# mLSTM projections: the o of heads 2 and 3 as one block of 512 columns, with its own order of token tiles

## The chip, the core and the metric

The kernel runs on one core of a Trainium2 chip as one program. A core has engines that run side by side, each through its own queue in order: TensorE (PE, matrix products; its weight loads are shown as PEld), VectorE (DVE), ScalarE (ACT), GpSimd (POOL) and SyncE (SP). SP and POOL here mostly issue DMA transfers between the device memory and the on-chip memory. TensorE writes its products to PSUM, from where ScalarE or VectorE must take them before the bank is used again. The metric is the device time of one execution in microseconds, the median over several runs.

## What is computed

A two-layer network over 1024 latent tokens and 256 context tokens, 1280 rows of width 1024. The first layer has neighbourhood attention heads beside four bidirectional mLSTM heads of dimension 256; the second has HGRN2 heads. The change touches only the mLSTM part of the first layer, whose reference is, cut to what matters:

```python
qa, ka, va, za, qb, kb, vb, ob, zb, g = _split_cols(h @ w_in, AB_SIZES)   # ob, zb: 1024 columns, 256 a head
hb_l, hb_c = _mlstm_bidir(mb_l, mb_c, need_ctx)          # two scans over chunks, forwards and backwards, summed
def merge(oa, hb, za, ob, zb):
    hb = jnp.swapaxes(hb, 1, 2) * jax.nn.sigmoid(_heads(ob, ML_HEADS))
    hb = _rms(hb, h_norm.reshape(ML_HEADS, ML_DIM))
    yb = hb.reshape(hb.shape[:2] + (ML_WIDTH,)) * jax.nn.silu(zb)
    ...
    return jnp.concatenate([ya, yb], axis=-1) @ w_out
```

So for each head the recurrence gives an h, which is gated by the projection o, normalized, and gated again by the projection z. o and z of a head are needed only when a token tile of its h is finished.

## The kernel before

**Projections.** The modulated input h stands transposed in on-chip memory as a high part and a low part (hh, hl), and so do the weights (`wblock`, L77 to L111: each piece of 128x512 is loaded by SP into one of three raw buffers `wraw`, L100, then ScalarE casts the high part, L71, and VectorE subtracts to get the low part, L72). `dense` (L124 to L130) makes each product of three matmuls per block of 128 rows of the inner dimension: high by high (L127), low by high or high by low (L128, L129). With an inner dimension of 1024 that is 24 matmuls for a tile.

A narrow block, `proj_out` (L304), projects onto 256 columns, one head. Its weights are four pieces. It takes two token tiles of 128 rows into one PSUM bank, 48 matmuls of 256 columns, evicts both at once, and POOL stores 256 KB to `md` (L319). Its order of tiles is the pairs that begin with 8, 4, 2, 6, 0. A wide block, `proj_wide` (L274), projects onto 512 columns, two heads side by side. Its weights are eight pieces: six go into the ring `w` of six slots, two into the ring `wx` of two slots. It takes one token tile at a time, 24 matmuls of 512 columns, evicts it and stores the halves for the two heads (L289). In both, the eviction goes through the ring `ev` of two buffers; for o it is a tanh on ScalarE (`gate_o`, L323), for z a tanh and a multiplication on VectorE (`gate_z`, L327), for v a copy (L283). Both use the two PSUM banks `mm`.

`ml_ahead(part, h, pool)` (L338) chooses: with a pool a part other than q and k is projected wide for heads h and h + 1, without one it is narrow. `md` holds v, o and z of the four heads.

**Recurrence.** `ml_rec` (L499) runs for the four heads one after the other, and `ml_load` of the next head is woven in. A head has ten chunks of 128 tokens in two directions: 20 steps, 80 in all. A step's first matmul is L534 (acc from mSD), the others are L544 (acc from mqc and the state mC) and L553 (the state's update from mvw), all of 258 columns. VectorE and ScalarE make mSD, mqc, mvw and update mC in between. Each tile of tokens is finished when the second direction has passed it: the forward direction goes 8, 9, 0, 1, ... 7, the backward one 9, 8, 7, ... 0, so the tiles are finished as 9, 8, 4, 3, 5, 2, 6, 1, 7, 0. For a finished tile `ml_out` (L593) loads o and z from `md` (L596, two buffers `mloz`, SP), gates by o (L599, VectorE), squares (L602, ScalarE), takes the root on GpSimd (L153, L155), scales and gates by z (L604, L605). `ml_yt` (L607) then transposes it (L612, TensorE; L613, ScalarE) and stores it to `yd` for the output projection.

**Output projection.** `out_ahead` (L835) makes the first half of the inner dimension (the attention heads' part of y, ready long before) for the second 512 output columns, ten token tiles of 24 matmuls of 512 columns (L829 to L831, in `out_sum`). Its weights use the six `w` slots and two slots `wo`; the `wo` slots, and its y pieces but for the first tile, stand where hh and hl stood, so they wait for the last projection. y of its first tile is loaded into the `ev` buffers (L812) and split into `wx` slots. Then `out_tile` (L847) adds the second half.

**Who sets the order.** The program is written in the order above, but a scheduler decides in which order the instructions stand on each engine's queue. It takes what is ready by its own timeline, highest priority first. Projections inside `with self.filler()` have a priority behind everything else, so they are placed into the gaps that the recurrence leaves on TensorE. Among themselves they keep the order of the program: v of heads 0 and 1 wide, z of head 1, v of heads 2 and 3 wide, o of head 2, z of head 2, o of head 3, z of head 3 (L1224 to L1229). On the chip each engine runs its queue in the order so fixed.

Of the kernel before, what the change touches and what calls it, by code (L numbers as in the profile page):

```python
# [43 lines left out]
class Prog:  # L44
# [293 lines left out]
    def ml_ahead(self, part, h, pool=None, mark=False):  # L338
        i = "qkvoz".index(part)
        c0 = (4 + i) * D + h * 256  # L340
        gate = {"o": self.gate_o, "z": self.gate_z}.get(part)
        if part in "qk":
            self.proj_out_tr(c0, self.mt[4 * i + h])
        elif pool:
            pair = self.md[4 * (i - 2) + h : 4 * (i - 2) + h + 2]
            self.proj_wide(c0, lambda s: pair[:, s, :].rearrange("h p f -> p h f"), pool, [8, 9] + list(range(8)), gate)
        else:

            self.proj_out(c0, self.md[4 * (i - 2) + h], gate, (8, 4, 2, 6, 0), mark)
# [762 lines left out]
    def build(self):  # L1112
        tc, nc, a = self.tc, self.nc, self.a
        dma = nc.sync.dma_start
        with ExitStack() as es:
# [88 lines left out]
            with tc.tile_pool(name="na", bufs=2) as pool, self.pp.phase(tq=1, s=2, acc=1):  # L1204
                qk = self.na_qk(0, pool)
                z = self.na_z(0, pool)
                ahead = [("k", 0), ("q", 1), ("k", 1), ("q", 2), ("k", 2), ("q", 3)]
                for p2 in range(8):
                    self.na_attn(p2, qk, z, pool)
                    if p2 < 7:  # L1210
# [5 lines left out]
                        z = self.na_z(p2 + 1, pool)  # L1216
# [5 lines left out]
            with tc.tile_pool(name="ml", bufs=2) as pool, self.pp.phase(s=2, acc=2):  # L1222
                with self.filler():
                    self.ml_ahead("v", 0, pool)  # L1224
                    self.ml_ahead("z", 1)
                    self.ml_ahead("v", 2, pool)
                    for h in (2, 3):
                        for part in "oz":
                            self.ml_ahead(part, h)  # L1229
                self.mask = self.t(pool, [P, 2, P], F32, "mmask", 1)  # L1230
                dma(out=self.mask, in_=a["mmask"])
                st, parts = self.ml_load(0, pool)
                for ld in parts:
                    ld()
                for h in range(4):
                    nxt, parts = self.ml_load(h + 1, pool) if h < 3 else (None, None)
                    self.ml_rec(h, st, pool, parts)
                    st = nxt

                ys = [self.out_y(0, 0, self.yd, pool, 2, (self.wp, "ev", 2), "wx")]  # L1240
                right.close()

                wr = es.enter_context(ExitStack())
                yp = wr.enter_context(tc.tile_pool(name="oy", bufs=1, side="right"))
                wo = (yp, "wo", 8)
                acc, w2 = self.out_ahead(
                    a["woab"], NT, self.yd, yp, ([(self.wp, "w", 6)] * 6 + [wo] * 2, [wo] * 8),
                    [[self.wp, 3, "wraw"]] * 2, ys,
                )
# [59 lines left out]
            with l1:  # L1309
                pool = l1.enter_context(tc.tile_pool(name="hg", bufs=2))  # L1310
# [3 lines left out]
                for h in range(16):  # L1314
# [5 lines left out]
                    z = st["z"]  # L1320
# [11 lines left out]
            with tc.tile_pool(name="op1", bufs=2) as op, ExitStack() as wl:  # L1332
# [3 lines left out]
                for b, w in ((1, w2), (0, w1)):  # L1336
                    self.gate_bc(1, op, 1, b)
                    for tt in range(8):
# [3 lines left out]
                            part=acc[:, tt, :] if b else None,  # L1342
# [142 lines left out]
```

## Time and profile before

| | us |
|---|---|
| runs of before: median, lowest, highest of 3 | 3489.57, 3488.38, 3491.35 |
| the profiled execution: its time, its span | 3489.28, 3487.5 |
| recurrence and fillers, about | 1150 to 1620 |
| first output projection (`out_ahead`) begins | 1622.8 |

The profile is of one execution. Times count from the start of its span. A row of the timeline gives start, length, engine, line, operation, out<-in, shapes, a count, and in brackets the idle time of the engine before it and what ended that. TensorE records of 258 columns come twice for each matmul in the program. TensorE's records overlap, since the matmuls are pipelined, so a matmul's price is read from the distance of starts, not from its length. PEclk is the share of the full TensorE clock that was granted.

### The profile page before, as it was taken

Reading aid. Unit: us, or ns where it says so; the run is one execution under the profiler, and the core shown is the slowest. Engines: PE = TensorE matmul, PEld = TensorE weight load, DVE = VectorE, ACT = ScalarE, POOL = GpSimd, SP = SyncE. Lnnn points to the kernel's source line nnn. Section 1 sums busy time; section 2 is a strip of 40 time slices with the busy share of each in tenths; the row PEclk is TensorE's granted clock in tenths of the full one; section 3 lists DMA queues with packets and bytes.
Section 4 is the critical chain, followed back from the end, with each engine's and each line's share of the span. In section 5 each row is a group of like instructions: output and inputs, shape, how many; then the busy total and the mean of one; then the engine's idle time right before and its main releaser. Section 6 shows DMA issues by size and latency. Waiting matters only on the chain.

```text
span 3487.5 us, 61004 instructions
## 1 busy us (share of the span) xinstructions
PE 3451.0 (99%) x23004; PEld 3073.9 (88%) x23004; DVE 2229.8 (64%) x5407; ACT 1478.8 (42%) x3557; POOL 522.5 (15%) x824
## 2 busy tenths in 40 slices
PE   8999999999999999999999999999999999999999
PEld 5679998889989888997888999999999999999887
DVE  4546665666655566886566666666666667666753
ACT  5445554555443444554354333333333333333431
POOL 2222222222211112222000000000100000100000
PEclk9999999999999999999999999999999999999999
DMA  5542222322233433434752111111111111111263
GB/s 204 173 134 57 82 77 72 91 80 76 78 90 101 140 118 122 138 120 148 215 166 67 37 37 34 37 37 37 35 36 35 35 36 37 37 36 33 85 195 116
DMA packets 321029, 303.98 MB, mean 87 GB/s; under 512 B 28168, under 2 KB 277192, under 8 KB 320736
## 3 DMA queue, kind: packets, MB, share of 16 engines
q1 hardware_dynamic: 288576, 216.47, 21.2%
q0 software_dynamic: 32160, 83.61, 7.1%
q8 instruction: 182, 2.98, 0.4%
q14 instruction: 111, 0.91, 0.1%
HBM read 240.52 MB, written 59.30 MB: 86 GB/s over the span
## 4 chain that ended last, share of the span: by engine, by line
PE 88%; issue 5%; DMA 3%; DVE 1%; ACT 1%; POOL 1%; SPq 0%; POOLq 0%; ACTq 0%; DVEq 0%
PE mm L128 19%; PE mm L127 19%; PE mm L129 19%; PE s L1015 5%; PE acc L772 2%; PE tr L752 2%; PE mm L829 2%; PE mm L830 2%; PE mm L831 2%; PE s L553 2%; PE acc L544 2%; PE acc L534 1%; PE acc L1075 1%; PE acc L1077 1%; PE acc L1076 1%
## 5 line engine op out<-in xcount | busy, mean ns | idle before, releaser
L128 PE MATMUL mm<-hl,wh 128*128 128x512 f32 (+1 forms) x1600 | 587.8, 367 | 0.0
L127 PE MATMUL mm<-hh,wh 128*128 128x512 f32 (+1 forms) x1600 | 584.1, 365 | 0.0
L129 PE MATMUL mm<-hh,wl 128*128 128x512 f32 (+1 forms) x1600 | 583.2, 365 | 0.0
L129 PE MATMUL mm<-wh,hl 128*128 128x256 f32 (+1 forms) x1620 | 496.6, 307 | 0.3 <-DVE hl L261 0.3
L127 PE MATMUL mm<-wh,hh 128*128 128x256 f32 (+1 forms) x1620 | 495.0, 306 | 1.4 <-ACT ev L316 0.6
L128 PE MATMUL mm<-wl,hh 128*128 128x256 f32 (+1 forms) x1620 | 495.4, 306 | 0.0
L129 PEld LDWEIGHTS mm<-hh,wl 128*128 128x128 f32 x1600 | 301.6, 189 | 45.7 <-issue 0.6
L127 PEld LDWEIGHTS mm<-hh,wh 128*128 128x128 f32 x1600 | 301.3, 188 | 45.2 <-issue 0.2
L128 PEld LDWEIGHTS mm<-hl,wh 128*128 128x128 f32 x1600 | 301.7, 189 | 43.3 <-issue 0.2
L127 PEld LDWEIGHTS mm<-wh,hh 128*128 128x128 f32 x1620 | 305.9, 189 | 15.1 <-issue 1.1
L128 PEld LDWEIGHTS mm<-wl,hh 128*128 128x128 f32 x1620 | 306.0, 189 | 13.6 <-issue 2.9
L129 PEld LDWEIGHTS mm<-wh,hl 128*128 128x128 f32 x1620 | 305.8, 189 | 13.7 <-issue 1.4
L127 PE MATMUL mm<-wzh,hh 128*128 128x256 f32 x1024 | 299.1, 292 | 0.4 <-ACT gz L921 0.4
L129 PE MATMUL mm<-wzh,hl 128*128 128x256 f32 x1024 | 291.5, 285 | 0.0
L128 PE MATMUL mm<-wzl,hh 128*128 128x256 f32 x1024 | 291.5, 285 | 0.0
L71 ACT CAST wh<-wraw 128x512 fp32r<-128x512 f32 x242 | 148.5, 620 | 242.8 <-PE mm L128 187.6
L72 DVE TENSOR_TENSOR wl<-wraw,wh 128x512 fp32r<-128x512 f32 x242 | 165.5, 689 | 93.0 <-ACT wh L71 82.6
L1015 PE MATMUL s<-gQ,gksel 128*128 128x128 f32 x1536 | 204.2, 276 | 0.0
L1010 ACT COPY gksel<-gK 128x512 f32<-128x512 f32 x192 | 120.3, 635 | 183.9 <-PE s L1015 152.7
L127 PEld LDWEIGHTS mm<-wzh,hh 128*128 128x128 f32 x1024 | 193.9, 189 | 0.6 <-ACT gz L921 0.6
L128 PEld LDWEIGHTS mm<-wzl,hh 128*128 128x128 f32 x1024 | 193.4, 189 | 0.0
L129 PEld LDWEIGHTS mm<-wzh,hl 128*128 128x128 f32 x1024 | 192.4, 188 | 0.0
(359 smaller groups left out, 7721.7 us busy)
## 6 DMA issues: line engine op xcount, KB each, us to landing
wraw<-yd SPq DMA_DIRECT2D x142, 256.0 KB
wraw<-in_wab_dram SPq DMA_DIRECT2D x112, 256.0 KB
wraw<-in_wc_dram SPq DMA_DIRECT2D x96, 256.0 KB
adar<-in_wada_dram POOLq DMA_DIRECT2D x32, 512.0 KB, 4.4
wraw<-in_wc_dram SPq DMA_DIRECT2D x128, 128.0 KB
md<-ev POOLq DMA_DIRECT2D x60, 256.0 KB, 2.9
mloz<-md SPq DMA_DIRECT2D x40, 256.0 KB
adar<-in_wada_dram SPq DMA_DIRECT2D x16, 512.0 KB
```

The costliest lines, as they stand in the source:

```text
L71: nc.scalar.copy(hi, x)
L72: nc.vector.tensor_tensor(out=lo, in0=x, in1=hi.bitcast(F32), op=ALU.subtract)
L127: mm(ps, lhsT=lh(k), rhs=rh(k), start=(k == 0), stop=False)
L128: mm(ps, lhsT=lh(k), rhs=rl(k), start=False, stop=False)
L129: m = mm(ps, lhsT=ll(k), rhs=rh(k), start=False, stop=(k == nk - 1))
L544: nc.tensor.matmul(num, lhsT=qc[:, j, :], rhs=C[d][:, j, :], start=False, stop=(j == 1))
L553: nc.tensor.matmul(u, lhsT=st["k"][c][:, j * P : (j + 1) * P], rhs=vw, start=True, stop=True)
L752: nc.tensor.transpose(pt[:nk, i, :], pr[:, o : o + nk], self.ident)
L772: m = nc.tensor.matmul(yp[h64], lhsT=v[:, h64], rhs=pTs[hd][:nk, i, :], start=(i == turn[0]), stop=(i == turn[-1]), tile_position=(0, hd * ...
L829: mm(ps, lhsT=yh[k], rhs=w.h(kk), start=(kk == 0), stop=False)
L1010: nc.scalar.copy(ksel.rearrange("p (b s i) -> p b s i", s=2, i=h), pick(K))
L1015: nc.tensor.matmul(pa[:, c, :].rearrange("p (b s i) -> p b s i", s=2, i=h), lhsT=ksel[:, c * P : (c + 1) * P], rhs=qp[:, c * nbc : (c + 1) ...
```

## The change

The o of heads 2 and 3 becomes one wide block of 512 columns, placed before z of head 2 and z of head 3, which stay narrow. The order of fillers behind v of heads 2 and 3 is then: o of both heads, z of head 2, z of head 3. And a wide block that is not v takes the token tiles as 8, 9, 4, 3, 5, 2, 6, 1, 7, 0 instead of 8, 9, 0, 1, ... 7. No z is projected with a pool, neither before nor after, so the wide o block is the only one with the new order. Two lines are added above the changed call, so lines from there on are two higher in the changed kernel.

```diff
         elif pool:
+
+            order = [8, 9] + (list(range(8)) if part == "v" else [4, 3, 5, 2, 6, 1, 7, 0])
             pair = self.md[4 * (i - 2) + h : 4 * (i - 2) + h + 2]
-            self.proj_wide(c0, lambda s: pair[:, s, :].rearrange("h p f -> p h f"), pool, [8, 9] + list(range(8)), gate)
+            self.proj_wide(c0, lambda s: pair[:, s, :].rearrange("h p f -> p h f"), pool, order, gate)
...
                     self.ml_ahead("v", 2, pool)
-                    for h in (2, 3):
-                        for part in "oz":
-                            self.ml_ahead(part, h)
+                    self.ml_ahead("o", 2, pool)
+                    self.ml_ahead("z", 2)
+                    self.ml_ahead("z", 3)
```

## The prediction

> **What bounds the kernel now.** First the page: the busy shares, then the chain that ended last.
>
> ```profile
> span 3487.5 us, 61004 instructions
> PE 3451.0 (99%) x23004; PEld 3073.9 (88%) x23004; DVE 2229.8 (64%) x5407; ACT 1478.8 (42%) x3557; POOL 522.5 (15%) x824
> PE 88%; issue 5%; DMA 3%; DVE 1%; ACT 1%; POOL 1%; SPq 0%; POOLq 0%; ACTq 0%; DVEq 0%
> ```
>
> TensorE is busy nearly everywhere, so the change is worth the matmul time that it takes out, and the TensorE idle time that it closes or opens. Busy time by stretches shows how much there is (columns: stretch, its length, then PE, PEld, DVE, ACT, POOL busy, the granted clock, the DMA share, GB/s):
>
> ```profile
> 1204.00:1616.40 412.40, 411.95 (x2538) 372.05 (x2536) 298.65 (x972) 194.21 (x514) 93.91 (x208) 1.00 0.38 117
> 1616.40:1622.80 6.40, 0.35 (x2) 0.17 (x2) 4.66 (x13) 3.50 (x7) 1.16 (x2) 0.84 0.87 258
> 1622.80:1627.60 4.80, 4.80 (x11) 3.60 (x12) 3.42 (x5) 2.48 (x4) 0.30 (x1) 0.50 1.08 377
> 1627.60:1690.00 62.40, 62.40 (x274) 50.42 (x274) 32.49 (x56) 33.32 (x66) 4.93 (x9) 1.00 0.67 201
> ```
>
> For 412 us, which hold nearly the whole mLSTM recurrence and its filler projections, TensorE lacks 0.45 us. Then comes one hole of 6.4 us, followed by 4.8 us at half clock. Who ended the waits of TensorE, from 1150 to 1640 us (columns: in total, times, longest):
>
> ```profile
> PE mm L829 <- ACT wxh L71: 3.3, 1, 3.3
> PE tr L612 <- ACT myt L613: 2.8, 1, 2.8
> PE mm L127 <- ACT wh L71: 0.4, 1, 0.4
> PE tr L464 <- DVE mkT L496: 0.4, 1, 0.4
> PE acc L544 <- DVE mqc L540: 0.4, 1, 0.4
> PE mm L128 <- DVE wxl L72: 0.2, 1, 0.2
> ```
>
> The hole is the passage from the last filler, z of head 3, to the output projection (L829 to L831):
>
> ```profile
> 1614.91 2.76 SPq L100 DMA_DIRECT2D wraw<-in_woab_dram  x3
> 1615.02 0.47 PE L129 MATMUL mm<-wh,hl 128*128 128x256 f32 x1
> 1617.72 0.43 SPq L812 DMA_DIRECT2D ev<-yd  x1
> 1619.19 0.33 PE L612 MATMUL tr<-ident,mhs 128*128 128x128 f32 x1 [2.82 <-ACT myt L613]
> 1622.11 0.62 ACT L71 CAST wxh<-ev 128x512 fp32r<-128x512 f32 x1
> 1622.78 0.80 PE L829 MATMUL mm<-wh,wxh 128*128 128x512 f32 x1 [3.26 <-ACT wxh L71]
> 1627.65 0.40 PE L829 MATMUL mm<-wh,wxh 128*128 128x512 f32 x1
> ```
>
> Weight slots come free as z of head 3 uses its weights for the last time; then three output weight pieces are loaded, and behind them on SP's queue the first y piece, whose cast at 1622.11 releases TensorE. From the start of the last z matmul to the first output matmul pass 7.76 us.
>
> **The change part by part.** *Matmuls.* Two blocks of 10 token tiles by 24 matmuls of 256 columns go (480), and 240 of 512 columns come. A matmul's price is the distance between starts inside a run:
>
> ```profile
> 1299.66 0.40 PE L128 MATMUL mm<-wl,hh 128*128 128x512 f32 x1
> ...
> 1302.23 0.40 PE L127 MATMUL mm<-wh,hh 128*128 128x512 f32 x1
> ...
> 1440.53 0.28 PE L127 MATMUL mm<-wh,hh 128*128 128x256 f32 x1
> ...
> 1441.94 0.28 PE L127 MATMUL mm<-wh,hh 128*128 128x256 f32 x1
> ...
> 1443.09 1.03 PE L553 MATMUL s<-mvw,mkn 128*128 128x258 f32 x4
> 1443.96 0.27 PE L612 MATMUL tr<-ident,mhs 128*128 128x128 f32 x1
> ```
>
> Between the first pair lie 12 matmuls of 512, 11 steps: 2.57/11 = 0.2336 us. Between the second 13 of 256, 12 steps: 1.41/12 = 0.1175 us. The last two give 0.2175 us for one record of a 258-column recurrence matmul, which has two: 0.435 us. So 480 x 0.1175 = 56.4 against 240 x 0.2336 = 56.1: **0.3 us less**; with 0.01 us of rounding in each difference, between 0.3 us more and 0.9 us less. Half the width costs half the time, so halving the count is worth hardly anything. 240 weight loads go too:
>
> ```profile
> L127 PEld LDWEIGHTS mm<-wh,hh 128*128 128x128 f32 x1620 | 305.9, 189 | 15.1 <-issue 1.1
> ```
>
> One takes 189 ns, more than the 117.5 ns between starts, so they overlap and cost nothing now.
>
> *Evictions, stores, weight loading.* Ten evictions of 128x512, ten stores of 256 KB, eight weight loads of 256 KB, eight casts and eight subtractions stand in both versions: 0. What differs is when: a wide block needs all eight pieces within its first tile, a narrow one four. In the trace the loading of o of head 2 runs so:
>
> ```profile
> 1380.01 6.58 SPq L100 DMA_DIRECT2D wraw<-in_wab_dram  x6
> 1382.91 0.62 ACT L71 CAST wh<-wraw 128x512 fp32r<-128x512 f32 x1 [2.25 <-DMA wraw<-in_wab_dram]
> 1383.56 0.69 DVE L72 TENSOR_TENSOR wl<-wraw,wh 128x512 fp32r<-128x512 f32 x1 [1.13 <-ACT wh L71]
> 1384.62 0.28 PE L127 MATMUL mm<-wh,hh 128*128 128x256 f32 x1
> ```
>
> Three raw buffers exist. The fourth piece is issued at 1380.01 and cast at 1382.91 (2.9 us); its raw buffer is free at 1384.25, so the seventh piece is ready about 1384.25 + 2.9 + 0.62 + 0.69 = 1388.5, the eighth some 1.3 us later. In the built order of the changed kernel, 7.6 and 8.7 us of matmuls lie between the last use of their two slots (the last six matmuls of v, about 1383 to 1384.4) and their first low-part use: about 1391 and 1393. Two to three microseconds of cover: 0. If it is gone, the price is what the first wide v block paid, the waits on wh, mkT and wxl above, 0.44 + 0.40 + 0.23 = 1.1 us.
>
> *z of head 2 comes later.* It now stands behind both o's. Counting the 80 recurrence steps (one L534 matmul each), its first pair of tiles ends after step 47 instead of 44. DVE works in order, so a late z holds it at L599, with the next recurrence matmuls behind it:
>
> ```profile
> 1611.49 0.43 DVE L599 SCALAR_TENSOR_TENSOR mhs<-mloz,mhs 128x256 f32<-128x256 f32 x1 [2.81 <-DMA mloz<-md]
> 1612.31 1.14 PE L544 MATMUL acc<-mC,mqc 128*128 128x258 f32 x4 [0.35 <-DVE mqc L540]
> 1614.80 0.42 DVE L605 TENSOR_TENSOR mhs<-mhs,mloz 128x256 f32<-128x256 f32 x1
> ...
> DMA to landing us min/median/max: 2.5/2.9/5.4
> ```
>
> (The last line is for the stores of this stage.) I measure each margin by the matmuls in the built order between the last one of the z tile and the first one that needs DVE work queued behind L599. Before, the two tightest are 43 of 256 and 12 of 258 columns, 10.3 us, without a wait, and 39 and 12 with five small ones, 10.4 us, with the 0.35 us wait above. After, the tightest is 46, 13 and four: 11.9 us; the next 15. So 0 is taken, and the 0.35 us goes, since z of head 3 now ends some 30 us ahead of need. If stores and loads took 5.4 instead of 2.9 us, 15.4 would be needed and about 3.5 us lost.
>
> *The passage moves into the recurrence.* This is the main term. In the built order of before, z of head 3 ends after step 80: nothing but two transposes and one matmul lies between it and the output projection. After, it ends behind step 69; eight 258-column matmuls (8 x 0.435 = 3.5 us) stand before the first output matmul, and the last eleven steps are interleaved with the first seven output tiles. If the 7.76 us stay, less the z matmul and 3.5 us of cover, 4.1 us are idle. SP's order puts the y loads ahead of the last weight load rather than behind it, which saves about one of the three issues above, 2.76/3 = 0.9 us. Bounds: 0 (y and weights already there) and 6.1 us (the cover works in vain). I take **3.5 us**, from the row that is the same passage.
>
> Before lost 0.35 + 2.82 + 3.26 us there, and at half clock 11 starts from 1622.78 to 1627.65 took 4.87 instead of 11 x 0.2336 = 2.57 us, 2.3 more: 8.7 us in all. With an idle stretch about half as long, broken by recurrence matmuls, I take it that the clock holds. The clock rule is a rival below.
>
> *Sum.* -0.3 - (8.7 - 3.5) = -5.5 us. The profiled execution took 3489.28 us around its span of 3487.5, so it would be 3483.8; the median of the runs shown is 0.29 higher: **3484.1 us**, -0.16%. A bound of 0.2%, about what a measurement of this kernel can tell from no change, is 7 us: 3482.6 and 3496.5.
>
> **The rivals.** *The passage is covered wholly*: recurrence matmuls fill the wait, since raw pieces are loaded ahead. All of 8.7 us is won: 3489.57 - 9.0 = 3480.6. For it: eleven steps are left. Against: TensorE takes its queue in order, so only the eight matmuls ahead of L829 help.
>
> *The half clock stays*: 3484.1 + 2.3 = 3486.4. For it: the windows above show 0.50 after a hole in which one transpose of 0.33 us ran. Against: the 0.35 us wait lies in the stretch that shows 1.00, so short waits do not do it. The Trainium skill (TensorE: Matmul & The Clock Gate, section on the HAM clock gate) says the half rate follows at least one idle activity window of about 3.4 us, with windows running freely. By that rule an idle stretch of 3.5 us would rarely fill a window and the clock would hold; the trace's transpose inside the halved window says that a window need not be quite empty.
>
> *The wait moves whole*: the recurrence matmuls ahead wait on DVE themselves, 6.1 us idle and 2.3 us half clock again; only 0.3 + 0.35 us are won: 3488.9.
>
> *Slower*: output matmuls and recurrence hold each other up. After, five loads of o and z for the last steps stand on SP's queue between the y loads of the output tiles, each waiting for a buffer that an earlier step frees.
>
> ```profile
> 1600.74 2.80 DMA mloz<-md
> ```
>
> One round costs this 2.8 us and the work from L599 to L605, 1611.49 to 1615.22, 3.7 us: 6.5 us. It decides where less than 6.5 us of matmuls lie between the freeing step and the y's use. Two such rounds and the half clock: 3484.1 + 13 + 2.3 = 3499.4. Against: in the built order 30 us and more lie between.
>
> That the change doesn't do what it says holds in part: no z is projected wide, so the new tile order serves only the one o block.
>
> **How the numbers follow.** Forecast 0.36, full cover 0.20, half clock 0.16, moved whole 0.12, slower 0.16. Faster: 0.20 and a third of the forecast's, 0.32; slower 0.16; same 0.52. The range runs from full cover with its matmul bound, 3480.6 - 0.6 = 3480, to the wait moved whole plus the late z and late weights, 3488.9 + 3.5 + 1.1 = 3493.5. The forecast's own range is 3481.5 to 3487.
>
> **What would show it.** Right: TensorE's wait on L829 shrinks to some 3.5 us and lies some 30 us earlier (eleven steps of about six 0.435 us matmuls), with recurrence steps behind it; no 0.50 clock; no wait on mqc L540 or myt L613; wide matmuls 0.234 us apart. Wrong: new TensorE waits on mSD, mqc or mvw of head 2 (late z), on wl or wxl at the start of the wide o, or on yh in the output tiles; or a hole as long as before.

## The result and the profile after

| kernel | median, us | runs | ratio to before, 95% interval |
|---|---|---|---|
| before, beside the changed kernel | 3489.57 | 14 | |
| changed kernel | 3482.77 | 14 | 0.9981 [0.9973, 0.9988] |
| its profiled execution, time and span | 3480.72, 3478.9 | 1 | |

The changed kernel is faster by 0.19%, between 0.12 and 0.27%: 4.2 to 9.4 us of 3489.57. The forecast was 5.5 us, which lies within this interval. A second chip gave 0.9978 (run `changed_again`, below). So the change is a gain, but the interval reaches to both sides of 0.2%.

First the page of the changed kernel: span, busy times, and the shares of the chain that ended last.

```profile
span 3478.9 us, 60541 instructions
PE 3447.0 (99%) x22764; PEld 3060.7 (88%) x22764; DVE 2230.8 (64%) x5407; ACT 1478.3 (42%) x3557; POOL 524.1 (15%) x824
PE 89%; issue 4%; DMA 2%; DVE 1%; ACT 1%; POOL 0%; SPq 0%; POOLq 0%; ACTq 0%; DVEq 0%
```

TensorE has 240 matmuls and 240 weight loads fewer (22764 against 23004), and its busy time fell by only 4 us, which includes what the half clock had cost before. The busy time by stretches (same columns as before: stretch, length, PE, PEld, DVE, ACT, POOL, granted clock, DMA share, GB/s):

```profile
1204.00:1560.00 356.00, 356.00 (x1993) 311.59 (x1992) 247.91 (x789) 166.83 (x436) 78.48 (x183) 1.00 0.41 124
1560.00:1600.00 40.00, 36.87 (x221) 32.80 (x220) 30.21 (x93) 20.39 (x50) 7.94 (x13) 1.00 0.57 179
1600.00:1640.00 40.00, 40.00 (x181) 33.40 (x180) 32.43 (x98) 19.82 (x49) 4.95 (x9) 1.00 0.40 116
```

There is still one hole, of 40 - 36.87 = 3.13 us instead of 6.1, and the row behind it shows a clock of 1.00 where before had 0.50. TensorE's waits from 1100 to 1800 us follow (in total, times, longest). `wxh` is the cast high part of y for the first output tile, `yh` that of the later tiles.

```profile
PE mm L831 <- ACT wxh L71: 3.1, 1, 3.1
PE mm L831 <- ACT yh L71: 1.0, 1, 1.0
PE mm L128 <- DVE wxl L72: 0.6, 1, 0.6
PE tr L466 <- DVE mkT L498: 0.3, 1, 0.3
```

The first line is the passage to the output projection (L831 is L829 of before). The second is new at its place, 1740 us; before had 0.3 us on `yh`, at 1698 us. The wait on `myt`, 2.8 us before, and the one on `mqc`, 0.4 us, are gone. The last two lie at 1168 to 1177 us, in the wide v block, ahead of the change. The passage in the timeline:

```profile
1585.05 0.28 PE L129 MATMUL mm<-wh,hl 128*128 128x256 f32 x1
...
1585.36 0.36 SPq L814 DMA_DIRECT2D wraw<-yd  x1
1585.78 0.50 SPq L814 DMA_DIRECT2D ev<-yd  x1
...
1588.24 0.70 PE L555 MATMUL s<-mvw,mkn 128*128 128x258 f32 x2
...
1591.40 0.62 ACT L71 CAST wxh<-ev 128x512 fp32r<-128x512 f32 x1 [0.19 <-DMA ev<-yd]
1592.08 0.50 PE L831 MATMUL mm<-wh,wxh 128*128 128x512 f32 x1 [3.13 <-ACT wxh L71]
```

The chain is the same as before: last z matmul, y's load, its cast, first output matmul. From 1585.05 to 1592.08 it takes 7.03 us instead of 7.76. Now eight recurrence matmuls, 3.8 us, run in its first half, and 69 of the 80 steps have begun at 1592.08, against all 80 before. The wait that is new comes 150 us later, behind these casts:

```profile
1738.58 0.62 ACT L71 CAST wh<-wraw 128x512 fp32r<-128x512 f32 x1 [7.28 <-DMA wraw<-in_wc_dram]
...
1739.38 1.37 ACT L71 CAST yh<-wraw 128x512 fp32r<-128x512 f32 x2 [0.18 <-DMA wraw<-yd]
```

ScalarE casts a weight piece of the next layer (`wc`), and only then the y that TensorE needs at once, at the second half of the output columns. Where the gain stands is read from two events, the first recurrence matmul and the first matmul of the next layer's scan, in before:

```profile
1189.75 0.60 PE L534 MATMUL acc<-mv,mSD 128*128 128x258 f32 x2
...
1896.08 0.53 PE L1015 MATMUL s<-gQ,gksel 128*128 128x128 f32 x3
```

and in the changed kernel:

```profile
1189.26 0.60 PE L536 MATMUL acc<-mv,mSD 128*128 128x258 f32 x2
...
1889.87 0.51 PE L1017 MATMUL s<-gQ,gksel 128*128 128x128 f32 x2 [0.72 <-ACT gksel L1012]
```

So 6.2 us are won by the scan, 0.5 of them already ahead of the recurrence. Between the two events, called the stage from here on, lie 706.3 us before and 700.6 after: 5.7 us less. The two profiled executions differ by 8.6 us; the other 2.4 come behind the first scan matmul, mostly from the last output stage, which the change doesn't touch. TensorE's waits from 3276 us on, before:

```profile
PE mm L829 <- ACT yh L71: 1.9, 2, 1.6
PE mm L829 <- DVE oacc L856: 1.7, 2, 0.8
PE mm L829 <- ACT woh L71: 1.1, 1, 1.1
```

and after:

```profile
PE mm L831 <- ACT yh L71: 1.5, 1, 1.5
...
PE mm L831 <- ACT woh L71: 0.4, 1, 0.4
PE mm L831 <- DVE oacc L858: 0.4, 1, 0.4
```

That is 4.7 us against 2.3. In other executions of the changed kernel and its relatives the same waits vary between 2.0 and 4.3 us. The time from the first scan matmul to the end is 1591.4 us in before and 1589.0 in the changed kernel, and over all fourteen traces of this study it lies between 1588.4 and 1591.4. So this part is taken as scatter between executions; the medians are 6.8 us apart.

### The profile page after: what moved, and what is told of

Read it like the earlier page. It is cut to its first block, busy times and chain, and to the rows that moved or that the text cites. A ratio compares the mean times of both kernels' runs of the same rounds, so it can differ in the third digit from the quotient of the medians.

```text
span 3478.9 us, 60541 instructions
## 1 busy us (share of the span) xinstructions
PE 3447.0 (99%) x22764; PEld 3060.7 (88%) x22764; DVE 2230.8 (64%) x5407; ACT 1478.3 (42%) x3557; POOL 524.1 (15%) x824
## 4 chain that ended last, share of the span: by engine, by line
PE 89%; issue 4%; DMA 2%; DVE 1%; ACT 1%; POOL 0%; SPq 0%; POOLq 0%; ACTq 0%; DVEq 0%
PE mm L128 19%; PE mm L129 19%; PE mm L127 19%; PE s L1017 5%; PE acc L774 2%; PE mm L831 2%; PE mm L833 2%; PE mm L832 2%; PE tr L754 2%; PE acc L546 2%; PE s L555 2%; PE acc L536 1%; PE acc L1077 1%; PE acc L1078 1%; PE acc L1079 1%
## 5 line engine op out<-in xcount | busy, mean ns | idle before, releaser
L127 PE MATMUL mm<-wh,hh 128*128 128x256 f32 (+1 forms) x1520 | 471.7, 311 | 0.9 <-ACT ev L316 0.6
L128 PE MATMUL mm<-wl,hh 128*128 128x256 f32 (+1 forms) x1520 | 470.6, 310 | 0.0
L129 PE MATMUL mm<-wh,hl 128*128 128x256 f32 (+1 forms) x1520 | 469.8, 309 | 0.0
L127 PEld LDWEIGHTS mm<-wh,hh 128*128 128x128 f32 x1520 | 287.3, 189 | 15.3 <-issue 0.9
L128 PEld LDWEIGHTS mm<-wl,hh 128*128 128x128 f32 x1520 | 287.3, 189 | 14.7 <-issue 3.0
L129 PEld LDWEIGHTS mm<-wh,hl 128*128 128x128 f32 x1520 | 287.1, 189 | 13.3 <-issue 1.5
```

The lines of the kernel that those rows point to most:

```text
L127: mm(ps, lhsT=lh(k), rhs=rh(k), start=(k == 0), stop=False)
L128: mm(ps, lhsT=lh(k), rhs=rl(k), start=False, stop=False)
L129: m = mm(ps, lhsT=ll(k), rhs=rh(k), start=False, stop=(k == nk - 1))
```

## The experiments

Two theories stood against each other. *Passage*: the gain comes from the passage to the output projection, which falls into the recurrence and is partly covered, so that the idle time shrinks and the clock holds. *Width*: the gain comes from the 240 matmuls and weight loads that the wide block saves, or from its order of tiles. All runs in one view; "before" is the kernel before on the same chip. The last column is the stage in the run's one profiled execution, 706.3 us in before and 700.6 in the changed kernel.

| run | median, us | before | ratio, 95% interval | stage, us |
|---|---|---|---|---|
| narrow_oozz | 3483.56 | 3489.94 | 0.9980 [0.9971, 0.9989] | 704.3 |
| narrow_late_steps | 3484.19 | 3489.94 | 0.9982 [0.9973, 0.9991] | 702.7 |
| wide_plain_order | 3483.22 | 3489.94 | 0.9981 [0.9972, 0.9990] | 701.6 |
| wide_z3_twice | 3514.89 | 3489.94 | 1.0070 [1.0056, 1.0084] | 734.3 |
| early_y | 3484.64 | 3489.35 | 0.9990 [0.9981, 0.9999] | 703.0 |
| early_y_narrow | 3482.89 | 3489.35 | 0.9983 [0.9974, 0.9992] | 700.8 |
| kept_busy | 3489.87 | 3489.35 | 1.0003 [0.9994, 1.0012] | 709.4 |
| wide_z | 3518.12 | 3489.35 | 1.0083 [1.0069, 1.0097] | 736.3 |
| wide_wc_later | 3481.56 | 3488.98 | 0.9978 [0.9969, 0.9987] | 698.4 |
| early_y_wc_later | 3478.93 | 3488.98 | 0.9967 [0.9955, 0.9980] | 699.4 |
| changed_again | 3482.28 | 3490.06 | 0.9978 [0.9969, 0.9987] | 699.8 |
| early_y_wc_later_again | 3479.27 | 3490.06 | 0.9969 [0.9956, 0.9981] | 698.4 |

### The same passage without the wide block

`narrow_oozz` is the kernel before with all blocks narrow and only their order changed, o, o, z, z.

```diff
-                    for h in (2, 3):
-                        for part in "oz":
+                    for part in "oz":
+                        for h in (2, 3):
```

> Only the order of the blocks is changed: both o's stay narrow (480 matmuls of 256 columns), in the order o of head 2, o of head 3, z of head 2, z of head 3. In the built order z of head 3 then ends behind step 66 of the recurrence, as early as in the changed kernel. Theory 'passage' (the gain comes from the passage to the output projection, which falls into the recurrence, has cover there and keeps the clock): 5 to 6.5 us faster than before, TensorE waits 2.5 to 4 us on the first output matmul, no stretch at clock 0.50. Theory 'width' (the gain comes from 240 fewer matmuls and weight loads and from the wide block's tile order): the time of before within 1 us.

Measured: 3483.56, within 1 us of the changed kernel, with 480 narrow matmuls. The output projection now starts behind 67 steps. Its waits from 1560 to 1760 us:

```profile
PE mm L829 <- ACT yh L71: 2.3, 1, 2.3
PE tr L612 <- ACT myt L613: 1.4, 1, 1.4
PE acc L534 <- ACT mhs L575: 0.3, 1, 0.3
```

The wait on `wxh` is gone, 1.7 us remain at the passage, and 2.3 us are lost at the start of the second half. By the medians the order of the fillers alone gives the gain. Two parts of the expectation missed: the wait at the passage is shorter than 2.5 us, and this execution has two stretches of 3.4 us at half clock, from 1588.1 and from 1745.1 us (the last section shows the first). Its stage is only 2.1 us shorter than that of before, so how the gain of the median comes about is not read from this trace.

`narrow_late_steps` keeps the order o, z, o, z of before and forces the last eleven steps behind the last projection: the first matmul of step 70, in head 3, may only come behind the last matmul of z of head 3.

```diff
+        self.last_mm = m
...
-                nc.tensor.matmul(num, lhsT=SD, rhs=st["v"][c], start=True, stop=(i == 0))
+                m = nc.tensor.matmul(num, lhsT=SD, rhs=st["v"][c], start=True, stop=(i == 0))
+                if (h, i, d) == (3, 4, 1):
+                    self.behind(m, self.last_mm)
```

> The kernel before with its own order of narrow blocks o, z, o, z; one ordering rule is added on TensorE alone: step 70 of the recurrence stands behind the last matmul of z of head 3, so that eleven steps are left behind the passage, as in the changed kernel. Theory 'passage': 4 to 6 us faster than before, wait on the first output matmul 2.5 to 4 us, clock 1.00 throughout. Theory 'width': the time of before or slower.

Measured: 3484.19, and in the trace from 1560 to 1760 us:

```profile
PE mm L832 <- DVE oacc L859: 2.4, 2, 2.1
PE mm L832 <- ACT wxh L71: 1.8, 1, 1.8
```

(`oacc` stands for the addition by which VectorE takes a tile's second half out of PSUM.) The passage loses 1.8 us, less than the 2.5 expected, the granted clock is 1.00 throughout, and 2.1 us are lost at a later tile. A third way to the same place gives the same time, and again some 2 us come up behind it.

### The order of the tiles

`wide_plain_order` is the changed kernel with the old order of tiles in the wide block.

```diff
-            order = [8, 9] + (list(range(8)) if part == "v" else [4, 3, 5, 2, 6, 1, 7, 0])
+            order = [8, 9] + list(range(8))
```

> The changed kernel with the wide o block in the tile order 8, 9, 0, 1, ... 7 instead of the order in which the tiles are finished. z of each tile comes later than o, so o's tile order binds nothing: the time of the changed kernel within 1 us, 6 to 7 us faster than before, the wait on the first output matmul again 3.1 us. If the tile order carries part of the gain, 2 us or more of it are lost here, with waits of VectorE on the loads of o and z in head 2.

Measured: 3483.22, wait on `wxh` 3.0 us. The new order of tiles is worth nothing that these runs can tell.

### The passage pushed back to the end of the recurrence

`wide_z3_twice` is the changed kernel with z of head 3 projected twice, which adds 240 narrow matmuls of unneeded work.

```diff
                     self.ml_ahead("z", 3)
+                    self.ml_ahead("z", 3)
```

> The changed kernel with z of head 3 projected and stored twice: 240 matmuls of 256 columns more, 240 x 0.1175 = 28.2 us of filler. In the built order this puts the passage behind step 80 again. Theory 'passage': beside the 28.2 us the hole and the half clock come back, 5.5 to 6.5 us, so 33 to 35 us slower than the changed kernel, 26.5 to 28.5 us slower than before, with a stretch at clock 0.50 after the hole. Theory 'width': 28 us slower than the changed kernel, 21 to 22 us slower than before.

Measured: 3514.89, 31.7 us above `wide_plain_order`. The added matmuls are worth 240 x 0.1175 = 28.2 us, which leaves 3.5 us: between the two theories' numbers, and with intervals of some 4 us on either side the time doesn't part them. The trace does: the stage is 734.3 us, 33.7 above the changed kernel and 28.0 above before, so that beside the added matmuls the whole gain is gone. All 80 steps are again ahead of the output projection, and from 1560 to 1760 us stand the two waits of before:

```profile
PE mm L831 <- ACT wxh L71: 3.2, 1, 3.2
PE tr L614 <- ACT myt L615: 2.7, 1, 2.7
```

with 6.8 us of half clock behind them, as before.

### The hole closed from the other side

If the hole is what matters, loading y of the first output tile earlier must close it whatever the fillers do. y is put into the raw ring of the weights instead of the eviction ring, whose buffers come free last. `early_y` does it in the changed kernel, `early_y_narrow` in the kernel before.

```diff
-                ys = [self.out_y(0, 0, self.yd, pool, 2, (self.wp, "ev", 2), "wx")]
+                ys = [self.out_y(0, 0, self.yd, pool, 2, (self.wp, "wraw", 3), "wx")]
```

> The changed kernel, but the y of the first output tile is loaded through the three raw buffers of the weights, behind z of head 3's pieces and ahead of the output weights, instead of through the two eviction buffers. It then lies split in its slots before z of head 3 ends, and in the built order the first output matmuls stand between the last ones of z. What the passage waited for was y (its cast ended the 3.1 us), so theory 'passage': the hole falls from 3.1 us to 1 us or less, 2 to 3 us faster than the changed kernel, 8.5 to 10 us faster than before. Rival: the hole is set by the weight slots that z of head 3 frees last; then the wait moves to the third weight piece and the time stays that of the changed kernel.

> The kernel before with the same early load of y and nothing else changed: narrow o's, order o, z, o, z. This prices the hole itself. Theory 'passage': the 2.8 and 3.3 us waits and the half clock go in good part, 5 to 8.5 us faster than before with no part of the change in the kernel. Theory 'width': at most 1 us.

Measured: in both the output projection no longer waits for the end of z. Its first matmul starts at 1579.67 us in `early_y` and at 1604.12 in `early_y_narrow`, each 0.12 us behind a matmul of z, and 10 and 12 us ahead of the last one. `early_y_narrow` won 5.9 us at the ratio's middle (2.8 to 9.1), as expected, with the old order of fillers and no part of the change: as much as the change itself. `early_y` won only 3.5 (0.3 to 6.6), not the 8.5 and more that were expected. Its waits from 1400 to 1760 us:

```profile
PE mm L831 <- ACT yh L71: 3.8, 2, 3.2
PE acc L536 <- ACT mhs L577: 1.0, 2, 0.6
PE acc L546 <- DVE mqc L542: 0.4, 1, 0.4
```

Of the 3.8 us 0.6 are what is left of the hole; the 3.2 are the wait at the second half, which was 1.0 in the changed kernel. So the hole shrank by 2.5 us, the wait 145 us later grew by 2.2, and 1.4 us of new waits came up in the recurrence. `early_y_narrow` has no wait above 0.6 us from 1100 to 1800 us.

### The clock kept up

`kept_busy` is the kernel before with twelve extra products into an unread PSUM tile behind the last recurrence matmul, to keep TensorE from idling. They show as 24 records, 5.34 us.

```diff
+                keep = self.ps("s", [P, 256])
+                for i in range(12):
+                    m = nc.tensor.matmul(
+                        keep, lhsT=self.ident, rhs=self.mask.rearrange("p d f -> p (d f)"), start=(i == 0), stop=(i == 11)
+                    )
+                    self.behind(m, self.last_rec)
```

> The kernel before with twelve matmuls of 256 columns of f32 that nobody reads, placed on TensorE behind the last recurrence matmul, in the hole, about 5.2 us. The passage itself is not shortened: some 7.8 us from the last z matmul to the first output matmul. Theory of the sum's term 'half clock': the clock stays at 1.00 behind the hole, 2.3 us faster than before (1.5 to 3). If an idle hole does not cause the half clock, or the half clock costs nothing: 0 +- 0.7 us.

Measured: 1.0003, between 2.1 us faster and 4.2 us slower, so the 2.3 us that were expected were not won. The stretches of the trace show what happened:

```profile
1616.40:1623.30 6.90, 5.60 (x28) 4.64 (x26) 4.94 (x15) 3.23 (x6) 0.91 (x2) 1.00 0.90 259
1623.30:1628.10 4.80, 4.62 (x19) 3.50 (x20) 3.43 (x5) 2.90 (x6) 0.43 (x1) 1.00 1.08 374
...
1697.75:1701.16 3.41, 1.21 (x6) 1.04 (x6) 3.09 (x6) 2.90 (x5) 0.57 (x1) 1.00 0.70 186
1701.16:1704.58 3.42, 3.42 (x9) 2.64 (x9) 3.04 (x6) 1.14 (x2) 0.00 (x0) 0.50 0.98 274
```

The clock did hold: in the 4.8 us behind the passage 19 matmuls ran where before had 11. But at 1697.8 TensorE then waited 2.2 us, a wait that before doesn't have, and the half clock came there, for 3.4 us, which costs 1.7. So some 2.3 us of faster matmuls were won, and 3.9 were lost 70 us later, in this one execution. Why the eviction (`oacc`, VectorE) was late there was not followed up.

### z wide as well

`wide_z` is the changed kernel with z of heads 2 and 3 as a wide block too.

```diff
-                    self.ml_ahead("z", 2)
-                    self.ml_ahead("z", 3)
+                    self.ml_ahead("z", 2, pool)
```

> The changed kernel with z of heads 2 and 3 as one wide block too, in the order in which the tiles are finished, so that the dormant part of the change acts. 480 matmuls of 256 columns become 240 of 512: 0.3 us. In the built order the passage falls behind step 60, with 3.1 us of recurrence matmuls ahead of the first output matmul. Theory 'passage': the time of the changed kernel within 1.5 us, wait on the first output matmul 3 to 4 us. Theory 'width': what the first halving gave comes again, 5 us or more faster than the changed kernel.

Measured: 3518.12, 28.8 us slower than before: a large miss. The projections end 22 us earlier and the output projection begins behind 60 steps instead of 69, but TensorE's waits from 1560 to 1780 us are now

```profile
PE mm L831 <- ACT wh L71: 13.5, 1, 13.5
PE mm L831 <- ACT yh L71: 12.3, 3, 6.6
```

and SP's queue from 1700 to 1772 us

```profile
SPq L854 <- DMA x<-ox: 16.4, 8, 5.5
SPq L814 <- DMA yd<-myt: 9.3, 1, 9.3
SPq L868 <- DMA yd<-myt: 6.3, 1, 6.3
```

and, in its timeline,

```profile
1748.52 15.16 SPq L854 DMA_DIRECT2D ox<-in_x_dram  x6
```

The output projection has run so far ahead that it asks for y tiles that the recurrence has not yet stored (`yd<-myt`). On SP's queue the loads of the residual (L854, two buffers, 15.16 us for six) come behind those waits, and behind these the next weights, whose cast TensorE awaits for 13.5 us. This chain is read from the order on the queue in one trace; no run takes a link out of it. It is a coupling through SP, as in the prediction's slower rival, but through other transfers: the rival had the loads of o and z (L598) in mind. SP does wait for their buffers, 36.7 us in six waits here and 23.4 us in eight in the changed kernel (both from 1560 to 1700 us), but there it makes no wait of TensorE that the profile shows.

### The wait at the second half, and a faster version

`wide_wc_later` and `early_y_wc_later` load the `wc` block, which stands ahead of the late y, behind the third tile instead. The first is made from the changed kernel, the second from `early_y`.

```diff
-                wf = [self.wring([a["wc"][:, 2048 : 2048 + P]], P), None]
+                wf = [None, None]
...
+                    if tt == 4:
+                        wf[0] = self.wring([a["wc"][:, 2048 : 2048 + P]], P)
```

> The changed kernel with one thing moved: the first wc weight block of the HGRN layer is loaded and cast behind the third tile of the second output half instead of ahead of the first. In the changed kernel's trace the matmul that starts this half waits 1.00 us for the cast of yh, which stands on ScalarE behind a cast of that weight block. Theory (the wait is made by that order of casts and loads): no wait above 0.3 us at that place, and about 1 us less than the changed kernel, 3481 to 3483; the gain itself is below what the timing can tell, so the trace decides. Rival (y itself lands late, its load being held on SP's queue by the residual loads ahead of it): the wait stays near 1 us and the time at 3482 to 3484.

> The kernel with the early load of y for the first output tile, and the first wc weight block loaded behind the third tile of the second output half. In the run with the early y alone the hole ahead of the output projection was 0.58 us instead of 3.13, but the wait at the second output half grew from 1.00 to 3.21 us. Theory (the late y there is pushed by the wc block ahead of it on SP's queue and on ScalarE): that wait falls below 1 us and the time to 3481 to 3482.5, 2 to 3 us below the early y alone. Rival (what is saved at the hole is waited for at the next place because the loads behind it are paced by their own chain): the wait stays at 2 to 3.5 us and the time at 3484 to 3485.5.

Measured: `wide_wc_later` has no wait left at that place, and its median is 3481.56, within the expectation. In `early_y_wc_later` the waits from 1400 to 1760 us are

```profile
PE acc L536 <- ACT mhs L577: 1.3, 2, 1.0
PE mm L831 <- ACT yh L71: 1.2, 1, 1.2
PE acc L546 <- DVE mqc L542: 0.3, 1, 0.3
```

The 1.2 us are what is left of the hole; the 3.2 us at the second half are gone, so it was the `wc` block that pushed the y, and the median is 3478.93, lower than the 3481 to 3482.5 expected. To set that beside the changed kernel on one chip, both ran again:

> The changed kernel once more, on the chip that also takes the next run, so that the two can be set side by side. Theory (the hole ahead of the output projection was worth about 6 us and closing it entirely brings some 3 more): 6 to 7 us below before, 3482 to 3483.5, with a wait of about 3 us on wxh and about 1 us on yh. Rival (the gain over the changed kernel seen in the run with the early y and the late wc block is spread between chips): the same time as the next run within 1 us.

> Early y of the first output tile and the wc block behind the third tile of the second half, as before. Theory (both waits of the changed kernel, 3.1 and 1.0 us, are cut to about 1.2 and 0 us in all, against 1.3 us of new small waits in the recurrence): 1.5 to 4 us below the changed kernel on the same chip, 3478.5 to 3481. Rival (no more than the changed kernel): 3482 to 3483.5.

Measured: the changed kernel 3482.28 (11 runs, 3480.42 to 3483.78), the version with both edits 3479.27 (5 runs, 3478.23 to 3480.57). Of the kernels here it has the lowest median, 10.8 us below before and 3.0 us below the changed kernel. What the early y adds to the late `wc` block is less sure: 2.6 us by the medians on one chip, nothing in the stages (698.4 us without it, 699.4 and 698.4 with it). Whether the old order of fillers with both edits would do as well was not tried.

## Why the prediction was right

*Matmuls, 0.3 us less.* In the changed kernel 7 steps of the wide stream, from 1400.08 to 1401.71 us, take 1.63 us: 0.233 each, as worked out. `narrow_oozz` and `narrow_late_steps` lie 0.3 and 1.0 us above `wide_plain_order` on the same chip, less than their intervals of some 3 us either way. So the runs don't speak against 0.3, but it is too small to be shown. The traces, one execution each, hint at more: TensorE's busy time in the stage is 699.5 us in before, 2.3 of it the cost of the half clock, and 695.8 in the changed kernel, which leaves 1.4 us. Where that comes from is open.

*Weights and eight pieces, 0.* No wait on `wh` or `wl` appears at the start of the wide o, and none on `wxl` there. Right.

*z of head 2 later, 0.* No wait on mSD or mvw, and the one on mqc (0.4 us before) is gone. Right; no run put z alone still later, so how much margin was left is not known.

*The passage.* Right in mechanism, place and size. The eight recurrence matmuls in front of the first output matmul are there and cover 3.8 us, where 3.5 was counted. Idle are 3.13 us where 3.5 was taken (the prediction's own terms, 4.1 - 0.9, give 3.2); in the second profile of the changed kernel 2.3. The passage became 0.73 us shorter; 0.9 was set down for the order on SP's queue. The way there was another in part: y's load into `ev` is issued 0.73 us behind the last z matmul where before it was 2.70, which is 2.0 us won, but its cast starts 5.6 us after the issue instead of 4.4, which takes 1.2 back. Why it took longer was not tried. The first output matmul comes 30.7 us earlier, with eleven steps behind it. The clock held, in both profiles of the changed kernel. The two narrow kernels that move the passage, `early_y_narrow`, which closes the hole with the old order, and `wide_z3_twice`, which brings it back, show that it is this and not the width. How much of the gain hangs on the clock is less sure: in the profiled execution of `narrow_oozz` it fell twice, yet its median shows the gain.

*The sum, and its luck.* By the traces the stage became 5.7 us shorter. TensorE's idle time in it went from 6.8 to 4.9 us, the half clock had cost 2.3, and the matmuls take the 1.4 to 1.5 us that remain. The sum had 5.2 for the first two terms, which brought 4.2: the late y at the second half, 1.0 us, was not foreseen, though `yh` in the output tiles was named as a sign of error, and 0.7 us came up at the first scan matmul. It had 0.3 for the matmuls, which brought more. That these errors cancel is luck, within the scatter of executions: the second profile of the changed kernel has 6.5 us less in the stage.

Whether all of the 8.7 us set down for the passage of before can be had is not settled. `early_y_narrow` closed it and brought 5.9, with an interval that reaches 9.1. `kept_busy` kept the clock at the passage, which the sum had at 2.3 us, and gained nothing, and in `early_y` most of what was saved at the hole was waited for at the second half. So the passage is not the only place that sets the end: the loads, casts and evictions behind it can take back what is saved ahead of them.

*The rivals.* Full cover and wait moved whole are excluded by the trace: 3.1 us of idle lie between 0 and 6.1. Half clock: 1.00 in all the rows behind the passage. Slower by SP: not here; `wide_z` ran into waits on SP's queue, by other transfers than the rival named.

## What to carry to other kernels

Where an engine is busy nearly always, price an edit by the one hole that it moves, not by the instructions that it saves: 240 matmuls in place of 480 of half the width were worth little (0.3 us by their spacing), moving the passage some 6 us, and one earlier load of y did as much without any new order. After closing a hole, look for the next queue on which the same kind of data arrive in order: in `early_y` 2.2 of the 2.5 us won at the hole were waited for 145 us later, until one weight load was moved out of the way. And a stage that starts earlier is a gain only as long as its inputs are there: with nine recurrence steps more left behind the passage, `wide_z` turned some 6 us of gain into 29 of loss.

## What was not expected of the hardware

The length of an idle stretch alone does not say whether the clock falls to half: an idle 2.2 us in `kept_busy` brought half clock, an idle 3.1 us in the changed kernel didn't. The clock fell behind a stretch of some 3.4 us in which TensorE was busy for 1.21 us in `kept_busy` (row shown above) and for 0.33 us in before:

```profile
1617.30:1620.80 3.50, 0.33 (x1) 0.14 (x1) 2.64 (x9) 1.99 (x4) 0.73 (x1) 0.99 0.75 217
```

Around half busy it went either way. The changed kernel has two stretches in its hole, both at 1.00 and followed by 1.00:

```profile
1587.30:1590.75 3.45, 1.65 (x7) 0.88 (x6) 1.45 (x4) 0.77 (x2) 0.73 (x1) 1.00 0.92 292
1590.75:1594.20 3.45, 2.12 (x9) 1.80 (x10) 3.45 (x11) 2.43 (x6) 0.00 (x0) 1.00 1.10 360
```

In `narrow_oozz` 1.69 us of work were followed by half:

```profile
1584.70:1588.10 3.40, 1.69 (x8) 0.85 (x7) 3.16 (x8) 3.40 (x10) 1.51 (x2) 1.00 0.94 278
1588.10:1591.50 3.40, 3.40 (x10) 2.66 (x10) 3.29 (x10) 2.09 (x5) 0.72 (x1) 0.50 1.06 325
```

The half clock lasted 3.4 us here and in `kept_busy`, 6.8 us in before. One can cut each trace into windows of 3.41 us that begin where one of its half-clock stretches begins. Over all fourteen traces, from 1100 to 3470 us, every such window at full clock with 1.45 us of TensorE work or less was followed by half clock, and none with 1.80 us or more. Between the two it held five times (1.50, 1.62, 1.63, 1.66 and 1.71 us) and fell four times (1.70, 1.72, 1.74 and 1.75).

The Trainium skill (TensorE: Matmul & The Clock Gate, section on the HAM clock gate) gives windows of about 3.4 us and asks for an idle one. The durations agree with such windows, the idle one does not: 1.21 and 1.69 us of work in one did not hold the clock.
